# The out-projection of a bidirectional SSD and Conformer layer, written as a software pipeline with a held order, and its state decay moved to ScalarE

## The chip, the cores and the metric

The kernel runs on one core of one Trainium2 chip. The time is that of one execution on the device, in microseconds (us); the median of several runs is compared. Before the change three runs took 1922.21, 1924.39 and 1927.9 us, median 1924.39 us.

## What is computed

One layer of a diffusion backbone over 2304 tokens of width 1024: 256 context tokens and 2048 latent tokens, 18 tiles of 128 tokens. Cut to what matters:

```python
h = rms_norm(x, g_pre) * (1 + scale) + shift
u = h @ w_in
z, xbc, dt_raw, ga, gb, gsil = jnp.split(u, ...)
y_ssd, h_fin = ssd_branch(z, xbc, dt_raw, ...)        # chunked scan, forward and backward, chunks of 128
  ...
  y = (y_f + flip(y_b) + d_skip * xs) * silu(z);  y = rms_norm(y, norm_g)
y_conf = conformer_branch(ga, gb, ...)                # depthwise conv, layer_norm, silu
y_conf = y_conf * silu(gsil)
out = concatenate([y_ssd, y_conf], -1) @ w_out        # 2048 -> 1024
return x + gate * rms_norm(out, g_post), h_fin
```

The backward scan of the SSD branch carries a state from each chunk to the one before it: `state = decay * state + increment`, and the chunk's output takes in `C^T state`. Everything is float32; products use a high and a low part (`h`, `l`) of each operand, so each product is three matmuls: high by high, high by low, low by high.

## The kernel before, in words

The kernel has two stages. The first and longer one makes the in-projection, the convolutions and the forward scan, and leaves per tile in DRAM: `YP` (the SSD output so far), `ZS` and `GS` (gates), `ST` (state increments), `EL` (decay rows), `XB` (the matrix C) and `CV` (the convolved Conformer branch). The second stage, from line 943, is the out-projection with the backward scan, and the change lies there.

The out-projection runs over the 18 tiles in the order 17, 16, ..., 2, 1, 0. For each tile `i` TensorE does 96 matmuls into two PSUM banks `op` (16 blocks `k` of the inner dimension, three products each, two halves of 512 columns; `out_part`, line 1088). Blocks 0 to 7 take the SSD half, `yh` and `yl`; blocks 8 to 15 the Conformer half, `ph` and `pl`. The weights are `woh0` to `woh15` and `wol0` to `wol15`; blocks 9 to 15 of them are loaded, cast and split (`load_wo`, line 952) at the stage's start, through staging buffers `wst` that share their memory with `yh` and `yl`.

What a tile needs ahead of its matmuls:

- SSD half (`ssd_pre`, line 975): loads `ct`, `elb`, `y`, `z`, `stl`; 8 matmuls `qo` of the state `Sb` by `ct`; VectorE multiplies by `elb` (line 993), adds to `y` (994), gates by `z` (995); ScalarE squares (996); VectorE sums eight slices to `zr` (970 to 972). GpSimd then multiplies the state by the decay `eTb` (1003) and adds the increment `stl` (1004).
- Conformer half: load `cn`; VectorE sums eight slices into `cs`; a matmul `cm` with ones spreads the sum over the partitions (1062); VectorE centres (1063); ScalarE squares (1068); VectorE sums to `nq`.
- Norms (lines 1013 and 1026): a matmul `pm` of `zr` and of `nq` by ones, VectorE's `yms`, GpSimd's power -1/2 (line 134), and a matmul `pn` that spreads the two factors over the partitions. VectorE scales `y` (1010) and `cn` (1074); ScalarE casts `yh` (1035), VectorE subtracts `yl` (1036); ScalarE makes eight Silu slices (1076), VectorE gates by `gsl` (1078), ScalarE casts `ph` (1084), VectorE subtracts `pl` (1085).
- Afterwards (`finish`, line 1096): ScalarE squares both `op` banks (1102), VectorE and GpSimd make the factor, VectorE scales (1109), adds the residual `xr` (1113), and SP stores.

The main loop (line 1156) writes these steps for the tile in work, for the next and for the next but one, among the 96 matmuls. The written order isn't what runs: the framework's scheduler orders each engine's instructions by its own forecast of the times, within the data dependencies and the number of buffers of each tag. On the chip every engine then works through its list strictly in that order. The SP queue does the same with the DMAs.

Of the kernel before, what the change touches and what calls it, by code (L numbers as in the profile page):

```python
# [65 lines left out]

@with_exitstack
def backbone_kernel(ctx, tc, xa, xt_in, cols, rows, wconv, conf_b, gp_row, bg_row, state0, w_mod, w_dt, w_in, w_out,
                    y_ctx, y_lat, new_state):
    nc = tc.nc  # L70
    V, S, G, T, DMA = nc.vector, nc.scalar, nc.gpsimd, nc.tensor, nc.sync
# [903 lines left out]
    def ssd_pre(i, first):  # L975
        ct = p1.tile([P, 2, P], F32, tag="ct", name=f"ct{i}", bufs=1)
        DMA.dma_start(ct, xb_slice(i, 10, 2))
        if not first:
# [8 lines left out]
        if not first:
            for g in range(2):
                gs = slice(4 * g, 4 * g + 4)
                po = bank("ss", f"qo{i}{g}")  # L990
                for q in range(4):
                    T.matmul(po[:, q * P:(q + 1) * P], Sb[g][:, q * P:(q + 1) * P], ct[:, g, :], start=True, stop=True)
                V.tensor_tensor(el[:, gs, :], el[:, gs, :], y8(po), MUL)
            V.tensor_tensor(y, y, el, ADD)
        V.tensor_tensor(y, y, z, MUL)
        S.activation(z, y, AF.Square)
        zr = sum8(p1.tile([P, P], F32, tag="zr", name=f"zr{i}", bufs=2), z[:, 0:4, :], z)
        for g in range(2):
            sg = st[:, g * 512:(g + 1) * 512]
            if first:  # L1000
                V.tensor_copy(Sb[g], sg)
            else:
# [29 lines left out]
    def ssd_hl(i, y):  # L1032
        yh = p0.tile([P, 8, P], F32R, tag="yh", name=f"yh{i}", bufs=2)
        yl = p0.tile([P, 8, P], F32R, tag="yl", name=f"yl{i}", bufs=2)
        S.copy(yh, y)  # L1035
        V.tensor_tensor(yl, y, yh.bitcast(F32), SUB)
        return yh, yl
# [20 lines left out]
    def conf_mean(i, n):  # L1058
        t = p2.tile([P, 4, P], F32, tag="cs", name=f"cs{i}", bufs=1)
        t = sum8(t[:, 0, :], t, n)  # L1060
        mean = bank("ss", f"cm{i}")[:, 0:P]
        T.matmul(mean, ones, t, start=True, stop=True)
        V.scalar_tensor_tensor(n, rows8(mean), -1.0 / D, n, MUL, ADD)
        return n

    def conf_square(i, n):
# [4 lines left out]
    def conf_act(i, n, v, pb):
        gs = p2.tile([P, 8, P], F32, tag="gs", name=f"gsl{i}", bufs=1)
        DMA.dma_start(gs, chan_slice(GS, i))
        V.tensor_tensor(n, n, rows8(pb[:, P:2 * P]), MUL)
# [4 lines left out]
        return v

    def conf_hl(i, v):
        ph = p2.tile([P, 8, P], F32R, tag="ph", name=f"ph{i}", bufs=1)
        pl = p2.tile([P, 8, P], F32R, tag="pl", name=f"pl{i}", bufs=1)
        S.copy(ph, v)
        V.tensor_tensor(pl, v, ph.bitcast(F32), SUB)
        return ph, pl

    def out_part(pso, hl, k0, k1, ns=(0, 1)):
        a, b = hl
        for k in range(k0, k1):  # L1090
            for m, (lhs, w) in enumerate(((a, WH[k]), (a, WL[k]), (b, WH[k]))):
                for n in ns:
                    T.matmul(pso[n], lhs[:, k % 8, :], w[:, n * 512:(n + 1) * 512],  # L1093
                             start=(k == 0 and m == 0), stop=(k == 15 and m == 2))

    def finish(i, pso, halves):
        x = p3.tile([P, D], F32, tag="xr", name=f"xr{i}", bufs=1)
        DMA.dma_start(x, xa[i * P:(i + 1) * P, :])
# [5 lines left out]
        V.tensor_scalar(ms[:, 0:1], ms[:, 0:1], 1.0 / D, EPS, MUL, ADD)
        r = rstd_of(p3, ms[:, 0:1], f"or{i}")
        g = gg[1 if i < NCTX else 0]
        for n in range(2):
            cs = slice(n * 512, (n + 1) * 512)
            V.scalar_tensor_tensor(o[:, cs], pso[n], r, g[:, cs], MUL, MUL)
            if halves:  # L1110
                V.tensor_tensor(o[:, cs], o[:, cs], x[:, cs], ADD)
        if not halves:
            V.tensor_tensor(o, o, x, ADD)
        dst = y_ctx[i * P:(i + 1) * P, :] if i < NCTX else y_lat[(i - NCTX) * P:(i - NCTX + 1) * P, :]
        for cs in (slice(0, 512), slice(512, D)) if halves else (slice(0, D),):
            DMA.dma_start(dst[:, cs], o[:, cs])

# [8 lines left out]
    yz = ssd_pre(i, False)  # L1126
# [27 lines left out]
    yz = ssd_pre(order[1], False)  # L1154
    n = conf_mean(order[1], conf_load(order[1]))
    for a, i in enumerate(order):
        last = a + 1 == NT
        nxt = None if last else order[a + 1]
        pt = conf_hl(i, v)
        banks(i)  # L1160
        if not last:
            v, nq = conf_square(nxt, n)
        out_part(pso[i], yh, 0, 2)
        if not last:
            rs = norms(nxt, yz, (v, nq))
        y = yz[0]
        if a + 2 < NT:
            n2 = conf_load(order[a + 2])
            yz = ssd_pre(order[a + 2], order[a + 2] == NCTX - 1)
# [8 lines left out]
        out_part(pso[i], pt, 9, 11)
        if a + 2 < NT:
            n = conf_mean(order[a + 2], n2)  # L1180
        if last:
            out_part(pso[i], pt, 11, 16, (0,))
            out_part(pso[i], pt, 11, 16, (1,))
        else:
            out_part(pso[i], pt, 11, 16)
# [1 line left out]
        if i == 1:
            load_gg(1)
        finish(i, pso[i], last)
# [61 lines left out]
```

## Time and profile before

| | |
|---|---|
| median of three runs | 1924.39 us |
| profiled execution: its time, its span | 1922.83 us, 1921.1 us |
| TensorE busy | 1827.8 us, 95% of the span, 11223 matmul records |
| VectorE, ScalarE, GpSimd busy | 1207.8, 799.6, 267.0 us |
| mean granted TensorE clock | 0.976 |
| longest group on the chain that ended last | `op`, line 1093, 18% of the span |

In rows of the profile PE is TensorE, PEld its weight load, DVE VectorE, ACT ScalarE, POOL GpSimd, SP the DMA queue's engine. A row of the timeline gives start, duration, engine, line, operation, output and inputs, the number of instructions merged, and in brackets how long the engine sat idle ahead and what released it. Matmul records overlap: the distance of the starts is what one costs. A row of a window gives its length, the busy time of each engine with the count of records, the granted clock (1.00 is full), the share of the DMA engines and GB/s. Some matmul records are missing.

### The profile page before, as it was taken

The page shows a single profiled execution, that of the slowest core. Times are in us where ns is not written, and L with a number is a line of the kernel's source. Part 1 is how long each engine was busy: PE and PEld are TensorE (multiplying, and loading weights), DVE is VectorE, ACT ScalarE, POOL GpSimd, SP SyncE. Part 2 cuts the span into 40 slices and gives each one's busy share as a digit, 9 for nine tenths or more (in the row PEclk, how much of TensorE's full clock was granted, in tenths as well). Part 3 has the DMA queues.
Part 4 walks back from the last instruction along what each step waited for, and adds up shares of the span by engine and source line. Part 5 has one row for each costly group of instructions (what it writes and reads, how often), then busy time and mean ns, then how long its engine had stood idle before and what let it go on. Part 6 is the DMA issues. An engine that isn't in the chain of part 4 may idle for free.

```text
span 1921.1 us, 29715 instructions
## 1 busy us (share of the span) xinstructions
PE 1827.8 (95%) x11223; PEld 1506.3 (78%) x11223; DVE 1207.8 (63%) x1807; ACT 799.6 (42%) x1684; POOL 267.0 (14%) x349
## 2 busy tenths in 40 slices
PE   7899999999999999999998899999988989898998
PEld 5788887787888888888876678778867877777776
DVE  2487978784555543587589555753367666757662
ACT  3656424454545432744245455642233332323331
POOL 0002001111101000100011111100123313323120
PEclk8899999999999999999999999999999999999999
DMA  8556666575666653555888888869666556456522
GB/s 302 202 208 218 220 205 201 193 255 168 235 204 205 223 189 122 195 175 179 214 201 227 218 226 260 244 197 288 232 188 185 155 143 181 130 142 174 166 70 73
DMA packets 305579, 375.34 MB, mean 195 GB/s; under 512 B 85270, under 2 KB 204950, under 8 KB 305436
## 3 DMA queue, kind: packets, MB, share of 16 engines
q1 hardware_dynamic: 284700, 335.69, 56.3%
q10 hardware_dynamic: 20736, 37.76, 6.8%
q8 instruction: 88, 1.44, 0.3%
q14 instruction: 55, 0.45, 0.1%
HBM read 243.79 MB, written 129.59 MB: 194 GB/s over the span
## 4 chain that ended last, share of the span: by engine, by line
PE 82%; DMA 6%; DVE 6%; issue 3%; ACT 2%; POOL 0%; SPq 0%; POOLq 0%; DVEq 0%; ACTq 0%
PE op L1093 18%; PE sp L377 7%; PE sp L378 7%; PE sp L379 7%; PE xp L377 5%; PE xp L378 5%; PE xp L379 5%; PE ga L377 3%; PE ga L379 3%; PE ga L378 3%; PE gb L377 3%; PE gb L379 3%; PE gb L378 3%; PE py L718 2%; PE po L725 2%
## 5 line engine op out<-in xcount | busy, mean ns | idle before, releaser
L682 ACT ACTIVATE lb<-lb,WB 128x128 f32<-128x128 f32 x576 | 184.7, 392 | 168.3 <-POOL lb L674 153.5
L377 PE MATMUL sp<-hh,wh 128*128 128x512 f32 (+1 forms) x640 | 238.5, 373 | 0.0
L378 PE MATMUL sp<-hl,wh 128*128 128x512 f32 (+1 forms) x640 | 236.2, 369 | 0.0
L379 PE MATMUL sp<-hh,wl 128*128 128x512 f32 (+1 forms) x640 | 236.0, 369 | 0.0
L674 POOL TENSOR_SCALAR_AFFINE_SELECT lb<-lb 128x512 f32<-128x512 f32 x144 | 111.7, 780 | 713.1 <-ACT el L671 349.1
L377 PE MATMUL xp<-hh,wh 128*128 128x512 f32 (+1 forms) x480 | 178.5, 373 | 5.1 <-ACT wh L352 2.9
L379 PE MATMUL xp<-hh,wl 128*128 128x512 f32 (+1 forms) x480 | 178.4, 372 | 0.0
L378 PE MATMUL xp<-hl,wh 128*128 128x512 f32 (+1 forms) x480 | 178.3, 372 | 0.0
L474 DVE SCALAR_TENSOR_TENSOR cva<-raw,cwh,cva 128x1280 f32<-128x1280 f32 (+1 forms) x96 | 141.7, 1484 | 18.1 <-ACT cva L468 16.0
L379 PEld LDWEIGHTS sp<-hh,wl 128*128 128x128 f32 x640 | 120.7, 189 | 20.7
L377 PEld LDWEIGHTS sp<-hh,wh 128*128 128x128 f32 x640 | 120.7, 189 | 20.5 <-DVE sth L554 0.2
L378 PEld LDWEIGHTS sp<-hl,wh 128*128 128x128 f32 x640 | 120.8, 189 | 19.7
L377 PE MATMUL ga<-hh,wh 128*128 128x512 f32 (+1 forms) x320 | 122.2, 382 | 5.7 <-DMA wh<-whd 5.7
L377 PE MATMUL gb<-hh,wh 128*128 128x512 f32 (+1 forms) x320 | 121.4, 379 | 6.4 <-DVE gth L541 6.4
L1093 PE MATMUL op<-woh,yh 128*128 128x512 f32 x288 | 95.7, 410 | 26.3 <-ACT yh L1035 26.1
L379 PE MATMUL ga<-hh,wl 128*128 128x512 f32 (+1 forms) x320 | 119.8, 374 | 0.5 <-DMA wl<-wld 0.5
L378 PE MATMUL ga<-hl,wh 128*128 128x512 f32 (+1 forms) x320 | 119.7, 374 | 0.0
L379 PE MATMUL gb<-hh,wl 128*128 128x512 f32 (+1 forms) x320 | 119.6, 374 | 0.0
L378 PE MATMUL gb<-hl,wh 128*128 128x512 f32 (+1 forms) x320 | 119.6, 374 | 0.0
L554 DVE SCALAR_TENSOR_TENSOR sth<-sth,sp 128x512 f32<-128x512 f32 (+1 forms) x80 | 50.5, 631 | 103.9 <-ACT sth L553 99.1
L377 PEld LDWEIGHTS xp<-hh,wh 128*128 128x128 f32 x480 | 91.6, 191 | 22.3 <-ACT wh L352 3.6
L594 DVE SCALAR_TENSOR_TENSOR cg<-cg,cv 128x256 f32<-128x256 f32 x240 | 107.8, 489 | 0.6
(224 smaller groups left out, 3820.6 us busy)
## 6 DMA issues: line engine op xcount, KB each, us to landing
lb<-lt ACTq DMA_DIRECT2D x144, 256.0 KB, 4.5
wr<-in_w_in SPq DMA_DIRECT2D x88, 256.0 KB, 4.6
whd<-wh SPq DMA_DIRECT2D x44, 512.0 KB, 3.4
wld<-wl SPq DMA_DIRECT2D x44, 512.0 KB, 5.6
wh<-whd SPq DMA_DIRECT2D x44, 512.0 KB, 4.9
wl<-wld SPq DMA_DIRECT2D x44, 512.0 KB, 5.7
xT<-xb SPq DMA_DIRECT2D x18, 512.0 KB, 5.4
yp<-yg SPq DMA_DIRECT2D x36, 256.0 KB, 4.3
```

What stands on the lines that cost most here:

```text
L377: T.matmul(ps[:, :BN], wh[:, k, :], hh[:, k, :], start=(k == 0), stop=False)
L378: T.matmul(ps[:, :BN], wh[:, k, :], hl[:, k, :], start=False, stop=False)
L379: T.matmul(ps[:, :BN], wl[:, k, :], hh[:, k, :], start=False, stop=(k == KT - 1))
L474: V.scalar_tensor_tensor(a[:, :n], raw[:, t:t + n], cwh[:, ct * 5 + t:ct * 5 + t + 1], a[:, :n], MUL, ADD)
L554: V.scalar_tensor_tensor(th, th, 1.0, ps[:, :BN], ADD, MUL)
L594: V.scalar_tensor_tensor(acc, g[:, t:t + 256], cv[:, w0 + t:w0 + t + 1], acc, MUL, ADD)
L674: G.affine_select(E[g, hq, d], E[g, hq, d], pattern=[[0, 4], [sg, P]], compare_op=ALU.is_ge, fill=NEG, base=0, channel_multiplier=-sg)
L682: S.activation(lb[:, h, :], lb[:, h, :], AF.Exp, bias=WB[:, i, c + h:c + h + 1])
L718: T.matmul(py[g][j * HD:(j + 1) * HD, q * P:(q + 1) * P], xt[g][:, h * HD:(h + 1) * HD], E[g, hq, 0][:, t, :], start=True, stop=True)
L725: T.matmul(po[g][:, q * P:(q + 1) * P], Sf[g][:, q * P:(q + 1) * P], bc[:, 2 + g, :], start=True, stop=True)
L1093: T.matmul(pso[n], lhs[:, k % 8, :], w[:, n * 512:(n + 1) * 512], start=(k == 0 and m == 0), stop=(k == 15 and m == 2))
```

## The change

Three things are done, all in the out-projection.

First, the steps are cut into smaller functions (`ssd_load`, `st_load`, `state_mm`, `state_decay`, `state_add`, `y_state`, `y_gate`, `y_sum`, `conf_sum`, `conf_centre`, `finish_squares`, ...), and the loop writes them out at chosen places among the matmuls. Matmuls of tile `i` carry beside them the norms, scaling, casts and Silu of the next tile, the state, gating and centring of the next but one, and the finish of the tile before. The loads of `ct`, `elb`, `y`, `z` and `cn` are written three tiles ahead.

Secondly, `V`, `S` and `T` become wrappers (`InOrder`): while `on` is set, which is in the main loop, the scheduler must keep each engine's instructions in the written order. GpSimd and the DMAs on SP stay free, and so does all that is written ahead of the loop.

Thirdly, the state's decay goes from GpSimd (one multiplication of 128x512 per half) to ScalarE (eight activations `Copy` of 128x64 with a scale per half, 16 a tile), and the addition of the increment from GpSimd to VectorE. GpSimd keeps the powers.

Buffers: `o` and `v` get two, `zr` and `nq` one, `ph` and `pl` stay at one; `cs` goes, its sums lie in `v`.

```diff
+class InOrder:
+    def __getattr__(self, name):
+        f = getattr(self._eng, name)
+        if not self.on:
+            return f
+        return lambda *a, **k: self._tc.keep_in_program_order(f(*a, **k))
...
-    V, S, G, T, DMA = nc.vector, nc.scalar, nc.gpsimd, nc.tensor, nc.sync
+    G, DMA = nc.gpsimd, nc.sync
+    V, S, T = (InOrder(tc, e) for e in (nc.vector, nc.scalar, nc.tensor))
...
-                G.tensor_tensor(b3(Sb[g]), b3(Sb[g]), bh(eTb[:, i, g * 8:(g + 1) * 8]), MUL)
-                G.tensor_tensor(Sb[g], Sb[g], sg, ADD)
+    def state_decay(i, g):
+        if i != NCTX - 1:
+            for h in range(8):
+                cs = slice(h * HD, (h + 1) * HD)
+                S.activation(Sb[g][:, cs], Sb[g][:, cs], AF.Copy, scale=eTb[:, i, 8 * g + h:8 * g + h + 1])
+    def state_add(i):
...
+                V.tensor_tensor(Sb[g], Sb[g], sg, ADD)
...
+    V.on = S.on = T.on = True
     for a, i in enumerate(order):
...
         banks(i)
+        pt = hl(p2, "p", 1, i, v)
+        out_part(pso[i], yh, 0, 1)
+        rs = None if last else norms(nxt, yz, nq)
+        if a:
+            finish_squares(order[a - 1])
+        lo(pt)
+        out_part(pso[i], yh, 1, 4)
+        if nxt is not None:
+            state_add(nxt)
+            pb = spread(nxt, rs)
+        if nx2 is not None:
+            st_load(nx2)
+            v2, t = conf_sum(nx2, n2)
+        if a:
+            finish_power(order[a - 1])
+        out_part(pso[i], yh, 4, 5)
+        if nx2 is not None:
+            state_mm(nx2)
+        if nxt is not None:
...
+            ssd_scale(nxt, y, pb)
+            yhn = hl(p0, "y", 2, nxt, y)
+            conf_scale(n, pb)
...
+            conf_silu(n, v)
+        out_part(pso[i], yh, 5, 8)
+        if nx2 is not None:
+            mean = conf_mean(nx2, t)
+        if nxt is not None:
+            lo(yhn)
+        if a:
...
+            finish_gate(order[a - 1])
+        out_part(pso[i], pt, 8, 10)
+        if nx2 is not None:
+            y_state(nx2)
+            state_decay(nx2, 0)
+            conf_centre(n2, mean)
+            conf_square(v2, n2)
+        if nxt is not None:
+            conf_gate(v, gs)
+        if nx2 is not None:
+            y_gate(nx2)
+            state_decay(nx2, 1)
+            gs = gs_load(nx2)
+            nq = conf_sqsum(nx2, v2)
+        if a:
+            finish_add(order[a - 1])
+        if nx2 is not None:
+            yz = y_sum(nx2)
+        if a + 3 < NT:
+            ssd_load(order[a + 3])
+            n, n2 = n2, conf_load(order[a + 3])
...
+            out_part(pso[i], pt, 10, 16)
```

Below, the numbers behind a name are the tile or block (`op10_0` is the first bank of tile 10, `yh9` the high part of tile 9) and a counter of the framework. On TensorE before the change, at the border of tile 10 and tile 9, the scheduler had put the spreading matmuls `pn9` between the last blocks of tile 10:

```order
L1093 MATMUL op10_1_15156<-wol14_13722,ph10_15151 128x512
L1029 MATMUL pn9_15246<-ident_209,yr90_15180 128x128
L1062 MATMUL cm8_15300<-cs8_15296,ones_218 128x128
L1029 MATMUL pn9_15246<-ident_209,yr91_15184 128x128
L1093 MATMUL op10_0_15155<-woh14_13723,pl10_15152 128x512
L1093 MATMUL op10_1_15156<-woh14_13723,pl10_15152 128x512
L1093 MATMUL op10_0_15155<-woh15_13729,ph10_15151 128x512
L1093 MATMUL op10_1_15156<-woh15_13729,ph10_15151 128x512
L1093 MATMUL op10_0_15155<-wol15_13728,ph10_15151 128x512
L1093 MATMUL op10_1_15156<-wol15_13728,ph10_15151 128x512
L1093 MATMUL op10_0_15155<-woh15_13729,pl10_15152 128x512
L1093 MATMUL op10_1_15156<-woh15_13729,pl10_15152 128x512
```

Eight matmuls of tile 10 stand behind `pn9`, and then the first matmul that reads `yh9`, which is made from `pn9`. After the change, in tile 9's own matmuls, `pn8` for the tile after stands behind block 3, and the state's product `qo7` behind block 4:

```order
L77 MATMUL op9_0_15480<-woh3_13142,yl9_15351 128x512
L77 MATMUL op9_1_15481<-woh3_13142,yl9_15351 128x512
L77 MATMUL pn8_15529<-ident_209,yr80_15496 128x128
L77 MATMUL pn8_15529<-ident_209,yr81_15500 128x128
L77 MATMUL op9_0_15480<-woh4_13168,yh9_15350 128x512
L77 MATMUL op9_1_15481<-woh4_13168,yh9_15350 128x512
L77 MATMUL op9_0_15480<-wol4_13167,yh9_15350 128x512
L77 MATMUL op9_1_15481<-wol4_13167,yh9_15350 128x512
L77 MATMUL op9_0_15480<-woh4_13168,yl9_15351 128x512
L77 MATMUL op9_1_15481<-woh4_13168,yl9_15351 128x512
L77 MATMUL qo70_15548<-ct7_15433,Sb0_13062 128x128 x4
L77 MATMUL qo71_15549<-ct7_15433,Sb1_13063 128x128 x4
```

`pn` has moved from 8 matmuls ahead of the tile that needs it to 72 ahead of it. The second place is the start of the out-projection on TensorE. Before, the first bank of tile 17 follows the last in-projection matmul `sp` at once:

```order
L379 MATMUL sp1_4640_7_4_13620<-hh4_7330,wl5536_1_13453 128x512
L1093 MATMUL op17_0_13783<-woh0_13065,yh17_13570 128x512
L1093 MATMUL op17_0_13783<-wol0_13064,yh17_13570 128x512
L1093 MATMUL op17_0_13783<-woh0_13065,yl17_13571 128x512
L1093 MATMUL op17_0_13783<-woh1_13091,yh17_13570 128x512
L1093 MATMUL op17_0_13783<-wol1_13090,yh17_13570 128x512
```

After, the small matmuls written ahead of the loop come first, and behind block 0 stands `pm16`, which needs the sums of tile 16:

```order
L393 MATMUL sp1_4640_7_4_13634<-hh4_7330,wl5536_1_13467 128x512
L1059 MATMUL pm17_13676<-ones_218,nq17_13672 128x1
L1070 MATMUL pn17_13682<-ident_209,yr171_13680 128x128
L1014 MATMUL qo160_13762<-ct16_13749,Sb0_13062 128x128 x4
L1014 MATMUL qo161_13763<-ct16_13749,Sb1_13063 128x128 x4
L1107 MATMUL cm16_13801<-v16_13797,ones_218 128x128
L77 MATMUL op17_0_13822<-woh0_13065,yh17_13584 128x512
L77 MATMUL op17_1_13823<-woh0_13065,yh17_13584 128x512
L77 MATMUL op17_0_13822<-wol0_13064,yh17_13584 128x512
L77 MATMUL op17_1_13823<-wol0_13064,yh17_13584 128x512
L77 MATMUL op17_0_13822<-woh0_13065,yl17_13585 128x512
L77 MATMUL op17_1_13823<-woh0_13065,yl17_13585 128x512
```

What could run at the start without tile 16, 48 matmuls of blocks 0 to 7 in the order before, is now 6 matmuls of block 0. On VectorE, in front of the sums for that `pm16`, the list after the change reads (`wol9` and `wol10` are the low parts of weight blocks 9 and 10):

```order
L1134 SCALAR_TENSOR_TENSOR v17_13594<-v17_13594,gsl17_13685 128x1024
L976 TENSOR_TENSOR wol9_13705<-wst9_13707,woh9_13706 128x1024
L976 TENSOR_TENSOR wol10_13711<-wst10_13713,woh10_13712 128x1024
L984 TENSOR_TENSOR v16_13797<-v16_13797 128x512
L984 TENSOR_TENSOR z16_13756<-z16_13756 128x512
L985 TENSOR_TENSOR v16_13797<-v16_13797 128x256
L985 TENSOR_TENSOR z16_13756<-z16_13756 128x256
L986 TENSOR_TENSOR nq16_13805<-v16_13797 128x128
L986 TENSOR_TENSOR zr16_13777<-z16_13756 128x128
L976 TENSOR_TENSOR wol11_13717<-wst11_13719,woh11_13718 128x1024
L77 TENSOR_SCALAR yms160_13836<-pm16_13833 128x1
L77 TENSOR_SCALAR yms161_13840<-pm16_13833 128x1
```

The gate of tile 17, which needs the load `gsl17`, and two weight splits now stand ahead of the sums of tile 16, and a third split ahead of `yms16`. Up to the last in-projection matmul TensorE's list is the same before and after, but for the name of one buffer.

More of the change, by code (lines that the diff above doesn't have):

```diff
@@ new lines, in st_load, with state_mm @@
+    def st_load(i):
+        sl[i]["st"] = p1.tile([P, D], F32, tag="st", name=f"stl{i}", bufs=1)
+        DMA.dma_start(sl[i]["st"], ST[i])
+    def state_mm(i):
+        if i != NCTX - 1:
+            sl[i]["po"] = [bank("ss", f"qo{i}{g}") for g in range(2)]
+            for g, po in enumerate(sl[i]["po"]):
+                for q in range(4):
+                    T.matmul(po[:, q * P:(q + 1) * P], Sb[g][:, q * P:(q + 1) * P], sl[i]["ct"][:, g, :],
+                             start=True, stop=True)
@@ L995, in ssd_pre, with y_sum @@
         V.tensor_tensor(y, y, z, MUL)
         S.activation(z, y, AF.Square)
[L997 to L1002, printed above, removed]
-                G.tensor_tensor(b3(Sb[g]), b3(Sb[g]), bh(eTb[:, i, g * 8:(g + 1) * 8]), MUL)
-                G.tensor_tensor(Sb[g], Sb[g], sg, ADD)
-        return y, zr
+    def y_sum(i):
+        z = sl[i]["z"]
+        zr = p1.tile([P, P], F32, tag="zr", name=f"zr{i}", bufs=1)
+        return sl[i]["y"], sum8(zr, z[:, 0:4, :], z)
@@ L1125, in backbone_kernel @@
     run(take(blocks, 5))
-    yz = ssd_pre(i, False)
+    ssd_load(i)
+    st_load(i)
+    state_mm(i)
+    y_state(i)
+    y_gate(i)
+    yz = y_sum(i)
+    for g in range(2):
+        state_decay(i, g)
+    state_add(i)
     run(take(blocks, 5))
@@ L1153, in backbone_kernel @@
     load_gg(0)
-    yz = ssd_pre(order[1], False)
-    n = conf_mean(order[1], conf_load(order[1]))
+    i = order[1]
+    ssd_load(i)
+    st_load(i)
+    n = conf_load(i)
+    state_mm(i)
+    y_state(i)
+    y_gate(i)
+    yz = y_sum(i)
+    for g in range(2):
+        state_decay(i, g)
+    v2, t = conf_sum(i, n)
+    conf_centre(n, conf_mean(i, t))
+    nq = conf_sqsum(i, conf_square(v2, n))
+    gs = gs_load(i)
+    ssd_load(order[2])
+    n2 = conf_load(order[2])
+    V.on = S.on = T.on = True
@@ L1156, in backbone_kernel @@
     for a, i in enumerate(order):
         last = a + 1 == NT
-        nxt = None if last else order[a + 1]
-        pt = conf_hl(i, v)
+        nxt = order[a + 1] if a + 1 < NT else None
+        nx2 = order[a + 2] if a + 2 < NT else None
         banks(i)
[L1161 to L1169, printed above, removed]
@@ L1184, in backbone_kernel @@
         else:
[L1185 removed]
+            out_part(pso[i], pt, 10, 16)
             yh = yhn
[L1187 to L1189 removed]
+    finish_squares(i)
+    finish_power(i)
+    finish_gate(i)
+    finish_add(i, True)
+    V.on = S.on = T.on = False
     state_out(1, Sb, lambda n: p1.tile([P, D], F32, tag="z", name=n, bufs=2)[:, 0:512])
```

144 lines of the change are left out of this document (81 added, 63 removed).

## The prediction

> **What bounds the kernel now.** I read the stretches first: the in-projection, the first two tiles of the out-projection, and its other sixteen, from the first matmul of tile 15 to the last of tile 0.
>
> ```profile
> 1100.00:1400.00 300.00, 300.00 (x2725) 241.79 (x2725) 163.98 (x244) 130.96 (x296) 36.72 (x42) 1.00 0.81 239
> 1402.30:1474.03 71.73, 57.37 (x268) 46.66 (x266) 53.91 (x66) 29.17 (x47) 21.37 (x18) 0.90 0.67 193
> 1474.03:1913.70 439.67, 409.71 (x1901) 342.01 (x1899) 277.11 (x384) 131.15 (x248) 108.95 (x98) 0.96 0.50 139
> ```
>
> After the length come the busy times of PE, PEld, DVE, ACT and POOL, then the granted clock. The in-projection has no gap on PE and the full clock. In the sixteen tiles PE is idle for 439.67 - 409.71 = 30.0 us, and the clock is below 1. The waits of PE in that stretch say for whom:
>
> ```profile
> PE op L1093 <- ACT yh L1035: 20.8, 9, 3.3
> PE op L1093 <- DVE yl L1036: 4.7, 2, 2.4
> PE op L1093 <- DVE oms L1104: 4.3, 2, 2.1
> ```
>
> So PE waits at the border of two tiles for the next tile's `yh` and `yl`. One border, on PE, shows the chain and what follows it:
>
> ```profile
> 1578.97 0.38 PE L1029 MATMUL pn<-ident,yr 128*128 128x128 f32 x2
> 1579.19 0.39 PE L1062 MATMUL cm<-cs,ones 128*128 128x128 f32 x2
> 1579.42 0.39 PE L1029 MATMUL pn<-ident,yr 128*128 128x128 f32 x2
> ...
> 1583.10 0.74 PE L1093 MATMUL op<-woh,yh 128*128 128x512 f32 x2 [2.83 <-ACT yh L1035]
> 1583.67 0.62 PE L1093 MATMUL op<-wol,yh 128*128 128x512 f32 x2
> 1584.14 0.28 PE L1018 MATMUL pm<-ones,zr 128*128 128x1 f32 x2
> 1584.28 3.57 PE L992 MATMUL qo<-ct,Sb 128*128 128x128 f32 x16
> 1587.50 0.90 PE L1093 MATMUL op<-woh,yl 128*128 128x512 f32 x2
> 1588.24 0.62 PE L1093 MATMUL op<-woh,yh 128*128 128x512 f32 x2
> ...
> 1591.88 0.39 PE L1093 MATMUL op<-woh,yl 128*128 128x512 f32 x1
> ```
>
> `pn` is done at 1579.6. VectorE then centres and scales, ScalarE casts, and at 1583.10 PE goes on. The product `qo` after the gap takes 3.22 us from start to start (1584.28 to 1587.50); without a gap ahead of it it takes 1.70:
>
> ```profile
> 1477.00 1.95 PE L992 MATMUL qo<-ct,Sb 128*128 128x128 f32 x16
> 1478.70 0.47 PE L1093 MATMUL op<-woh,yh 128*128 128x512 f32 x1
> ```
>
> PE is thus slowed to about half for some us after each stall. At full clock the 16 `op` matmuls from 1588.24 to 1591.88 cost 3.64 / 16 = 0.2275 us each. From the same rows `pn` costs 2 x 0.22, `cm` 0.23, `pm` 2 x 0.14. The sixteen tiles hold 1536 `op` (349.4 us), and in the order after 13 `qo` (22.1), 15 `pn` (6.6), 14 `cm` (3.2) and 15 `pm` (4.2): 385.5 us of work. Before, one `qo` more lies in the stretch, so its 439.67 are 387.2 of work, 30.0 of idling and 22.5 of slowed work.
>
> **The change, part by part.**
>
> *Steady tiles.* With `pn` behind block 3 the chain to the next `yh` has 72 matmuls, 16.4 us, of cover, where it had 8. What can be late next is the sum `zr` ahead of `pm`, because PE must now do `pm` behind block 0: behind a late `pm` 90 matmuls queue that don't need it. VectorE's list per tile, priced by starts in a stretch where GpSimd was idle:
>
> ```profile
> 1594.52 0.68 DVE L970 TENSOR_TENSOR cs<-cn 128x512 f32<-128x512 f32 x1
> 1595.12 1.21 DVE L1085 TENSOR_TENSOR pl<-v,ph 128x1024 fp32r<-128x1024 f32 x1
> 1596.25 1.21 DVE L995 TENSOR_TENSOR y<-y,z 128x1024 f32<-128x1024 f32 x1
> 1597.39 0.41 DVE L971 TENSOR_TENSOR cs<-cs 128x256 f32<-128x256 f32 x1
> 1597.72 0.68 DVE L970 TENSOR_TENSOR v<-v 128x512 f32<-128x512 f32 x1
> 1598.33 0.28 DVE L972 TENSOR_TENSOR cs<-cs 128x128 f32<-128x128 f32 x1
> 1598.53 0.41 DVE L971 TENSOR_TENSOR v<-v 128x256 f32<-128x256 f32 x1
> ```
>
> Nine of 128x1024 at 1.13 (10.2), seven of 128x512 at 0.60 with the two moved state additions (4.2), three tails of sums at 0.33 + 0.20 (1.6), the finish's two scalings (1.3) and four tiny ones (0.6): 17.9 us. The list starts when `pm` is read, at 1.9 us of the tile's clock. It waits some 0.7 for `pn` (on PE at 6.2) and 1.5 for ScalarE's casts and squares, so `zr` of the following tile is there at 22, and its `pm` is due at 24.5 + 1.4 = 25.9 (24.5 is 96 x 0.2275 and one `qo`, `pn`, `cm` and `pm`). Slack 4 us.
>
> ScalarE has 131.15 / 16 = 8.2 us of work per tile and gets 16 activations of 128x64. None is in the trace; the nearest rows bound it, one without and one with a per-partition operand:
>
> ```profile
> L444 ACT ACTIVATE lr<-pl 128x128 f32<-128x128 f32 x4 | 0.9, 268 | 1.1 <-DVE lr L443 1.1
> L682 ACT ACTIVATE lb<-lb,WB 128x128 f32<-128x128 f32 x576 | 184.7, 392 | 168.3 <-POOL lb L674 153.5
> ```
>
> At 0.27 to 0.39 us they add 4.3 to 6.3, and ScalarE holds 12.5 to 14.5 of 24.5 us; I take 0.35, nearer to the row with the operand. The first eight lie between Silu and the square that waits for the centring, the others after the last square, so at either end they stay covered by PE; without that cover they would cost their 5.6 us. GpSimd loses its state work; only its powers remain on the path, covered by blocks 1 to 3.
>
> SP's list per tile becomes `xr`, `z`, `stl`, `ct`, `y`, `cn`, `elb`, `gsl`, store, each waiting for a buffer.
>
> ```profile
> gsl<-gs SPq DMA_DIRECT2D x14, 512.0 KB, 6.1
> stl<-st SPq DMA_DIRECT2D x13, 512.0 KB, 6.1
> cn<-cv SPq DMA_DIRECT2D x13, 512.0 KB, 4.9
> ```
>
> By these landing times `stl` can leave at 4.5 (after the state additions) and is due at 27.8; `cn` leaves at 12 (after Silu) and is due at 28.9; `gsl` leaves at 16.2 and is due at 39. The least slack is 12 us. So the sixteen tiles cost no wait: 385.5 instead of 439.7, a gain of 54.2, of which 22.5 hang on the clock.
>
> [...]
>
> *The start.* It gets worse. The in-projection's last matmul gives way at 1402.3, where the second stretch begins. `pm17`, its power and `pn17` take 1.2 us, `qo16`, `cm16` and block 0 take 3.3: 1406.9. Then `pm16` waits for `zr16`, which stands on VectorE behind the gate of tile 17, which waits for `gsl17`, which waits for the last write of GS:
>
> ```profile
> 1403.86 5.41 DMA gs<-sth
> ...
> 1414.82 4.17 DMA wst<-in_w_out
> ...
> 1423.51 9.73 DMA wst<-in_w_out
> ```
> ```profile
> wst<-in_w_out SPq DMA_DIRECT2D x7, 512.0 KB, 7.8
> ...
> gsl<-gs SPq DMA_DIRECT2D x4, 512.0 KB, 5.9
> ```
>
> 1409.3, and 5.9 to land: 1415.2; gate 1.1, two weight splits 2.3, sums 2.3: `pm16` at 1421. PE idles 14 us where before it had 42 more matmuls to do and idled 5.2; and it starts slowly after a long gap:
>
> ```profile
> 1421.05 1.22 PE L1093 MATMUL op<-woh,ph 128*128 128x512 f32 x2 [5.18 <-ACT ph L1084]
> ...
> 1427.67 0.63 PE L1093 MATMUL op<-woh,ph 128*128 128x512 f32 x2
> ```
>
> (fourteen matmuls in 6.6 us there, some 3 us lost). Blocks 1 to 3 end at 1428. Meanwhile the staging buffers pass the weights one after another: wst11 leaves when `wol9` is made (1417.6), and load, cast and split take 7.8 + 2.3; so blocks 11, 13 and 15 are split at 1427.7, 1437.8 and 1447.9. `yms16` stands behind the first, `cm15`'s sums behind the second, `yl16` behind the third. PE gets through `pn16` at 1429.3, `cm15` at 1438.7, and ends tile 17 at 1449.6. Tile 16's block 0 ends at 1451; `zr15` comes 8.5 us of VectorE's list after `yl16` (1449.0), so `pm15` at 1457.6, a stall of 6.5 and 3 of slow clock, and tile 15 begins at 1483.5. If loads land in 4.2 us, PE's own work and one stall give 1472; at 9.7 us, 1489. I take 1482, near the median of the loads: 8 us later than the 1474.03 of before.
>
> *The end.* From the last matmul's start to the span's end it is 7.8 us in both orders (1913.33 to 1921.1):
>
> ```profile
> 1913.33 0.39 PE L1093 MATMUL op<-woh,pl 128*128 128x512 f32 x1
> ...
> 1917.52 0.94 SPq L1116 DMA_DIRECT2D out<-o  x2
> ```
>
> The final state's 8 transposes and two copies fall in there now, beside VectorE's last steps: 0 to 1 us, taken as 0.
>
> *The sum.* Span 1921.1 + 8 - 54.2 = 1874.9. The profiled execution took 1922.83 and lies 1.6 under the median of 1924.39; the same difference of 46.2 from the median gives 1878.
>
> **The rivals.**
>
> *Slowed work stays.* If something else than the gaps lowers the clock in this stage, the 22.5 us stay: 1878 + 22.5 = 1901. [...] Against it stand the 300 us without a gap at a granted clock of 1.00, and the slow `qo` right behind a gap.
>
> *A longer start.* The held lists couple the weight splits with the sums, and every load there competes. If each of the first two tiles loses one load more (9.7 us), tile 15 begins 20 us later: 1898. For it: the 71.73 us of the first two tiles already hold 14.4 of idling. Against: fewer than three loads in a row can stand ahead of any matmul.
>
> *VectorE's held list is late in each tile (slower).* Place: `pm`, behind block 0. If a load, a cast or GpSimd's power comes late, VectorE can no longer pass it, and `zr` comes after 25.9. Each us beyond is a us of PE's, and a stall of 2 us brought a slow stretch of 1.5 (the `qo` above). The loop's gain per tile is 54.2 / 16 = 3.4, less 0.5 for the start: a list 5.4 us longer than my 22, that is 27.4, eats all of it; at 29 us it is 16 x 1.6 = 26 us slower: 1950. Before, VectorE needed 277.11 / 16 = 17.3 us of work per tile and had free choice; that, and 4 us of slack, speaks against.
>
> *It does nothing.* The order might be held and the waits merely move, each tile's stall as long as now, at another matmul: 1924. The order on TensorE has moved, so this needs VectorE's list at just 27 us.
>
> **How the numbers follow.** Forecast 1878, chance 0.68; alone its range is 1866 to 1890 (start from -2 to +15, up to 5 us of small waits). Slowed work stays 0.07; longer start 0.14; VectorE late 0.06, of which 0.05 slower; nothing 0.05, of which 0.03 within 0.3%. A measurement of this kernel tells 0.3% (6 us) from no change. Faster by more: 0.92, within: 0.03, slower: 0.05. The range leaves out the slower cases and half of the 1901: 1864 to 1902.
>
> **What would show it.** Right: the sixteen tiles in 384 to 392 us, PE idle under 5 us in them, granted clock 1.00, `qo` at 1.7 throughout, no wait for `yh`; `pm16` waiting some 14 us at 1407 to 1421 and `pm15` some 6; ScalarE's activations of 128x64 at 0.27 to 0.39. Wrong: PE waiting at `pm` in each tile (VectorE's list over 25 us), at `qo` for the state (ScalarE's decay late), or a clock under 0.98 without gaps; or the first two tiles over 95 us.

## The result and the profile after

The changed kernel takes 1873.74 us (median of 4 runs, 1872.07 to 1875.25), the kernel before 1926.14 us beside it (1922.21 to 1928.67): a ratio of 0.9729, 95% interval 0.9708 to 0.9751. The forecast was 1878 us; as a gain it was 46 us, and 52 were measured. The profiled execution took 1872.28 us, its span is 1870.5 us (before 1922.83 and 1921.1), so the span has lost 50.6 us.

The windows of the changed kernel, with the columns of the prediction's table: the first two tiles, from the end of the in-projection's last matmul (by its row, 0.17 us after the next one starts) to the first matmul of tile 15, and the sixteen tiles from there to the start of the last matmul of tile 0.

```profile
1405.07:1472.40 67.33, 54.19 (x266) 45.60 (x266) 52.93 (x73) 41.45 (x96) 5.35 (x6) 0.90 0.77 206
1472.40:1862.61 390.21, 390.21 (x1892) 327.95 (x1891) 272.46 (x409) 178.96 (x453) 40.72 (x46) 1.00 0.55 155
```

The sixteen tiles have no idle PE left and the full granted clock, where before 30 us of idling stood at a clock of 0.96. All waits of PE behind the in-projection are now these two, both in the first tile:

```profile
PE pm L77 <- DVE zr L986: 12.3, 1, 12.3
PE pn L1070 <- POOL yr L148: 0.9, 1, 0.9
```

One tile on PE, from its `pm` to the next. (L77 is the line of the helper that holds the order; all held instructions bear it.)

```profile
1498.60 0.28 PE L77 MATMUL pm<-ones,zr 128*128 128x1 f32 x2
1498.74 0.36 PE L77 MATMUL pm<-ones,nq 128*128 128x1 f32 x2
1498.96 0.72 PE L77 MATMUL op<-woh,yh 128*128 128x512 f32 x2
1499.52 0.63 PE L77 MATMUL op<-wol,yh 128*128 128x512 f32 x2
...
1503.18 0.61 PE L77 MATMUL pn<-ident,yr 128*128 128x128 f32 x4
...
1505.02 1.95 PE L77 MATMUL qo<-ct,Sb 128*128 128x128 f32 x16
1506.72 0.70 PE L77 MATMUL op<-woh,yh 128*128 128x512 f32 x2
...
1523.44 0.28 PE L77 MATMUL pm<-ones,zr 128*128 128x1 f32 x2
```

The period is 1523.44 - 1498.60 = 24.84 us, and `qo` takes 1.70 (1505.02 to 1506.72). In the same tile VectorE is done with `zr` at 1518.75, 4.7 us ahead of `pm`, and until it can read `pm` it waits 5.22 us; ScalarE's eight decays of one half take 2.01 us:

```profile
1518.46 0.29 DVE L77 TENSOR_TENSOR zr<-z 128x128 f32<-128x128 f32 x1
1523.97 0.23 DVE L77 TENSOR_SCALAR yms<-pm 128x1 f32<-128x1 f32 x2 [5.22 <-PE pm L77]
```
```profile
1509.37 2.01 ACT L77 ACTIVATE Sb<-Sb,eTb 128x64 f32<-128x64 f32 x8
```

The start, on PE and on VectorE: `pm16` waits for `zr16`, which stands behind the gate of tile 17 (which waits for `gsl`) and two weight splits.

```profile
1422.20 0.56 PE L77 MATMUL pm<-ones,zr 128*128 128x1 f32 x2 [12.26 <-DVE zr L986]
1423.05 1.20 PE L77 MATMUL op<-woh,yh 128*128 128x512 f32 x2
...
1428.66 0.61 PE L77 MATMUL pn<-ident,yr 128*128 128x128 f32 x4
```
```profile
1416.28 1.23 DVE L1134 SCALAR_TENSOR_TENSOR v<-v,gsl 128x1024 f32<-128x1024 f32 x1 [3.70 <-DMA gsl<-gs]
1417.42 2.36 DVE L976 TENSOR_TENSOR wol<-wst,woh 128x1024 fp32r<-128x1024 f32 x2
...
1421.77 0.28 DVE L986 TENSOR_TENSOR zr<-z 128x128 f32<-128x128 f32 x1
```

Where the 50.6 us went, from start to start of the matmuls that bound the stages: the in-projection's last matmul started 2.6 us later (1404.67 for 1402.09), the first two tiles, from there, lost 4.2 (71.94 to 67.73), the sixteen tiles lost 49.1 (1913.33 - 1474.03 = 439.30 to 390.21), and the end, from the last matmul's start at 1862.61 to 1870.5, grew by 0.1. Sum: 2.6 - 4.2 - 49.1 + 0.1 = -50.6.

### The profile page after: what moved, and what is told of

Same layout as the page of the kernel before. It is cut to its first block, busy times and chain, and to the rows that moved or that the text cites. A ratio compares the mean times of both kernels' runs of the same rounds, so it can differ in the third digit from the quotient of the medians.

```text
span 1870.5 us, 30012 instructions
## 1 busy us (share of the span) xinstructions
PE 1808.1 (97%) x11223; PEld 1493.1 (80%) x11223; DVE 1203.1 (64%) x1841; ACT 863.8 (46%) x1956; POOL 175.9 (9%) x281
## 4 chain that ended last, share of the span: by engine, by line
PE 85%; DMA 7%; DVE 4%; ACT 1%; issue 1%; SPq 1%; POOL 0%; POOLq 0%; DVEq 0%; ACTq 0%
PE op L77 21%; PE sp L391 7%; PE sp L392 7%; PE sp L393 7%; PE xp L391 5%; PE xp L392 5%; PE xp L393 5%; PE ga L391 3%; PE ga L393 2%; PE ga L392 2%; PE gb L391 2%; PE gb L393 2%; PE gb L392 2%; DMA lb<-lt 2%; PE py L732 2%; DVE cg L608 2%
## 5 line engine op out<-in xcount | busy, mean ns | idle before, releaser
L391 PEld LDWEIGHTS sp<-hh,wh 128*128 128x128 f32 x640 | 120.6, 189 | 20.8 <-DVE sth L568 0.4
L392 PEld LDWEIGHTS xp<-hl,wh 128*128 128x128 f32 x480 | 91.7, 191 | 15.7 <-DVE hl L312 0.4
```

What stands on the lines that cost most here:

```text
L391: T.matmul(ps[:, :BN], wh[:, k, :], hh[:, k, :], start=(k == 0), stop=False)
L392: T.matmul(ps[:, :BN], wh[:, k, :], hl[:, k, :], start=False, stop=False)
```

## The experiments

**Which of the three parts pays.** Four kernels ask it. The first lets all three engines be ordered by the scheduler, with the loop as the change writes it:

```diff
-    V.on = S.on = T.on = True
+    V.on = S.on = T.on = False
```

> The changed kernel with its new loop and the decay on ScalarE, but with no engine held to the written order. TensorE's order is then, in a steady tile, pm behind the first four matmuls of the second half, pn 22 matmuls later, and 22 more, qo and cm ahead of the next tile's yh. Theory 'the loop as written' (the norms are asked for an iteration early, whoever orders them): from pm to yr the changed kernel's trace shows 2.9 us and from pn to yh 2.8 us; 22 matmuls cover 5.0 and 7.0 us, so the sixteen tiles stay at 385 to 400 us with less than 10 us of waiting for yh, and tile 17's first half is no longer behind pm16: 1860 to 1882 in all. Rival 'the held order': without it the borders wait as before the change (20 us for yh, some slowed work): 1900 to 1925.

Measured: 1880.33 us (1879.62 to 1882.06), ratio 0.979 (0.9769 to 0.9812). All its waits of PE behind the in-projection:

```profile
PE op L1141 <- ACT ph L1076: 7.4, 1, 7.4
PE op L1141 <- ACT yh L1076: 6.4, 2, 3.4
PE op L1141 <- DVE yl L1080: 3.7, 1, 3.7
```

These are four waits: three in the first two tiles (7.4, 3.4, 3.7) and one of 2.9 near the end; the tiles between have none. There the scheduler, given this loop, puts 22 matmuls, `qo` and `cm` between `pn` and the next `yh`, and the period is 24.98 us. So the loop as written, with its buffers and the decay on ScalarE, brings 40.6 us (1920.95 - 1880.33), and the rival falls. The buffers were not tested apart from the loop.

The second holds TensorE alone:

```diff
-    V.on = S.on = T.on = True
+    T.on = True
```

> The changed kernel with TensorE alone held to the written order; VectorE and ScalarE are ordered by the scheduler. Theory 'TensorE's order is what pays': VectorE has 5 us of slack at pm in each tile, so its order may shift by that much for nothing: 1868 to 1880. Rival 'VectorE must be held too': another order puts a step of the next tile behind one that waits, pm or yh then waits 2 us or more in each of 16 tiles and TensorE slows after each wait: 1900 or more.

Measured: 1873.79 us (1870.93 to 1874.58), ratio 0.9752 (0.9726 to 0.9778), within the spread of the changed kernel. Holding VectorE and ScalarE brings nothing; holding TensorE brings the 6.5 us between these two kernels. Their profiles say where. The first two tiles take as long in both (70.5 and 70.3 us from the last in-projection matmul to tile 15), though the waits differ. From tile 15 to the last matmul it is 396.1 us without and 390.8 with the order held, and 4.3 of these 5.4 lie in the last four tiles, where the wait of 2.9 is. The rest is the in-projection's end, 1.7 us later in the free kernel.

The third puts the state back on GpSimd, with all orders held:

```diff
-            for h in range(8):
-                cs = slice(h * HD, (h + 1) * HD)
-                S.activation(Sb[g][:, cs], Sb[g][:, cs], AF.Copy, scale=eTb[:, i, 8 * g + h:8 * g + h + 1])
+            G.tensor_tensor(b3(Sb[g]), b3(Sb[g]), bh(eTb[:, i, g * 8:(g + 1) * 8]), MUL)
...
-                V.tensor_tensor(Sb[g], Sb[g], sg, ADD)
+                G.tensor_tensor(Sb[g], Sb[g], sg, ADD)
```

> The changed kernel with all orders held, but with the state's decay and addition back on GpSimd. Theory 'the decay was not in the way': GpSimd's work of 6 us per tile slows VectorE while it runs (before the change 128x1024 steps beside the addition took 2.3 us where others took 1.2, some 3 us more per tile), less the 1.2 us of additions that VectorE loses; the 5.2 us for which VectorE waits at pm take that up, and the time stays at 1870 to 1880. Rival 'ScalarE's decay is needed': VectorE's list passes the slack or qo waits for the state, 2 us or more in each of 16 tiles: 1900 or more.

Measured: 1872.84 us (1871.93 to 1873.97), ratio 0.975 (0.9729 to 0.9771): no difference. GpSimd's addition and VectorE beside it, in one tile:

```profile
1509.92 3.53 POOL L1027 TENSOR_TENSOR Sb<-Sb,stl 128x512 f32<-128x512 f32 x2
```
```profile
1510.60 1.70 DVE L77 TENSOR_TENSOR y<-y,elb 128x1024 f32<-128x1024 f32 x1
...
1524.64 0.22 DVE L77 TENSOR_SCALAR yms<-pm 128x1 f32<-128x1 f32 x2 [5.03 <-PE pm L77]
```

One VectorE step is 0.5 us longer beside the addition (1.70, elsewhere 1.22), less than I expected from the 2.3 us of such steps before (at 1590.04 and 1592.29, beside additions from 1589.00 to 1593.51), and VectorE still waits 5.03 us for `pm`.

The fourth is the kernel before with the decay on ScalarE and the addition on VectorE, and nothing else:

```diff
-                G.tensor_tensor(b3(Sb[g]), b3(Sb[g]), bh(eTb[:, i, g * 8:(g + 1) * 8]), MUL)
-                G.tensor_tensor(Sb[g], Sb[g], sg, ADD)
+                for h in range(8):
+                    cs = slice(h * HD, (h + 1) * HD)
+                    S.activation(Sb[g][:, cs], Sb[g][:, cs], AF.Copy, scale=eTb[:, i, 8 * g + h:8 * g + h + 1])
+                V.tensor_tensor(Sb[g], Sb[g], sg, ADD)
```

> The kernel before with one part of the change only: decay on ScalarE, addition on VectorE. TensorE's order at the border of two tiles stays (pm, 22 matmuls, pn, 4 to 9 matmuls, then the wait). Theory 'the border's order bounds': the chain pn, centring, scaling, cast ran while GpSimd was idle, so the waits for yh stay at 20 us or more and the time within 10 us of the kernel before. Rival 'GpSimd's load was the bound': VectorE is relieved of the slow steps beside GpSimd and the gain is 20 us or more.

Measured: 1932.00 us (1925.36 to 1934.87) beside 1920.95, ratio 1.0047 (1.0028 to 1.0066): slower by 0.5%, by the medians 11 us, just past the 10 I had set. `yh` is waited for 33.2 us in the stretch of the sixteen tiles, where it was 20.8:

```profile
PE op L1095 <- ACT yh L1037: 33.2, 13, 3.3
```

One border shows one way. On VectorE `y` starts at 1617.34 and is done when the next step starts, at 1618.47; ScalarE has just begun seven decays, and the cast comes behind them:

```profile
1617.34 1.21 DVE L1012 TENSOR_TENSOR y<-y,pn 128x1024 f32<-128x1024 f32 x1
1618.47 1.22 DVE L1076 TENSOR_TENSOR cn<-cn,pn 128x1024 f32<-128x1024 f32 x1
```
```profile
1618.56 1.77 ACT L1005 ACTIVATE Sb<-Sb,eTb 128x64 f32<-128x64 f32 x7
1620.23 1.03 ACT L1037 CAST yh<-y 128x1024 fp32r<-128x1024 f32 x1
```

Seven of the 13 waits, 14.6 us together, have seven or more decays right ahead of the cast like this one. At the other six (18.6 us) no decay stands there. At five of these, 3.30 us each, the scheduler has put no `op` at all between `pn` and the next `yh`; before the change that was so at three borders:

```profile
1645.80 0.39 PE L1031 MATMUL pn<-ident,yr 128*128 128x128 f32 x2
1649.48 0.99 PE L1095 MATMUL op<-woh,yh 128*128 128x512 f32 x2 [3.30 <-ACT yh L1037]
```

So TensorE's order didn't quite stay, and the longer waits are in part the decays in front of the cast and in part another order of the scheduler. The move of the decay brings no gain here, and no difference where the loop leaves slack; it is not what pays.

**How much slack VectorE has.** The step that makes `yl` is repeated, four or seven times more:

```diff
-            lo(yhn)
+            for _ in range(5):
+                lo(yhn)
```

> The changed kernel with VectorE's subtraction that makes yl done five times instead of once in each tile (four more steps of 1.13 us, 4.5 us; the value is the same). In the changed kernel VectorE waits 5.2 us per tile for pm. Theory 'slack of 5 us': the list still ends ahead of pm, nothing waits: within 6 us of the changed kernel, 1868 to 1880. Rival 'no real slack' (something else on the list is already tight, such as the gate's load or the state): 2 us or more per tile, 1905 or more.

Measured: 1882.74 us (1880.77 to 1883.50), ratio 0.9783 (0.9755 to 0.981); a little above my bound. In the steady tiles the theory holds: `zr` ends just ahead of `pm`, and the period is 25.07 on average.

```profile
1631.14 0.29 DVE L77 TENSOR_TENSOR zr<-z 128x128 f32<-128x128 f32 x1
1632.13 0.22 DVE L77 TENSOR_SCALAR yms<-pm 128x1 f32<-128x1 f32 x2 [0.70 <-PE pm L77]
```

Most of what it costs stands in the start, where `pm15` waited 5.5 us for `zr` (in the changed kernel VectorE waited only 1.55 us for that `pm`): in the profiles the first two tiles are 8.6 us longer, and the sixteen 3.1.

> The same with seven more steps, 7.9 us per tile, 2.7 us beyond the slack: the place of my rival 'VectorE's held list is late'. Theory 'each us beyond is a us of TensorE's and the gap slows it': pm waits some 2.7 us in each of 15 or 16 tiles (40 us), and the 18 matmuls behind it take up to 1.5 us longer, which VectorE, waiting for pn, passes on: 1913 to 1940. Rival 'VectorE catches up' (the delay is taken back, since the steps wait for nothing else): under 1895. PE's waits should all stand at pm.

Measured: 1971.41 us (1969.61 to 1974.03), ratio 1.0246 (1.0216 to 1.0276): slower than the kernel before, and 31 us above my range. Every tile waits at `pm`:

```profile
PE pm L77 <- DVE zr L77: 64.2, 16, 8.0
```

One of these borders on PE, and what VectorE does with it:

```profile
1610.01 0.59 PE L77 MATMUL pm<-ones,zr 128*128 128x1 f32 x2 [3.76 <-DVE zr L77]
1610.89 1.20 PE L77 MATMUL op<-woh,yh 128*128 128x512 f32 x2
...
1617.06 0.60 PE L77 MATMUL pn<-ident,yr 128*128 128x128 f32 x4
```
```profile
1617.70 1.22 DVE L77 TENSOR_TENSOR y<-y,pn 128x1024 f32<-128x1024 f32 x1 [2.44 <-PE pn L77]
...
1620.04 10.04 DVE L77 TENSOR_TENSOR yl<-y,yh 128x1024 fp32r<-128x1024 f32 x8
```

The repeated steps took 10.04 / 8 = 1.25 us each, not 1.13, so 8.8 us were added, 4.1 beyond the slack of 4.7; the wait at `pm` is 3.8. Behind it the 18 matmuls up to `pn` took 6.2 us instead of 4.2, and VectorE, the late engine, waited 2.44 us for `pn` instead of 0.48. The tile takes 31.3 us (1610.01 to 1641.31 at the next `pm`): 24.84, 3.8 of waiting and 2.6 of slowed work, which comes back as lateness. I had priced the gap without most of that.

**Whether the gap slows what follows.** In these two, `pn` stands behind the tile's last matmul, and what needs it behind it; the second has PE work in the gap, on unused columns of the bank of `cm`:

```diff
-            pb = spread(nxt, rs)
...
+            out_part(pso[i], pt, 10, 16)
+        if nxt is not None:
+            pb = spread(nxt, rs)
```
```diff
+            if nx2 is not None:
+                for _ in range(22):
+                    T.matmul(cmb[nx2][:, 256:512], WL[0][:, 0:P], WL[0][:, 0:256], start=True, stop=True)
```

> The changed kernel with all orders held, but pn asked for behind the tile's last matmul instead of behind block 3, with the scalings and casts that need it behind it on VectorE and ScalarE. PE has nothing to do from pn to yh, some 2.6 us by the changed kernel's rows (pn to the scaling 0.65, scaling 1.2, cast 1.1, less pn's own 0.44), then 0.3 for yl, in 16 tiles: 46 us. Theory 'a gap slows what follows': another 1.5 us per tile, 1935 to 1950. Rival 'a gap costs its own length': 1915 to 1925. Rival 'the place of pn doesn't matter': under 1890.

> The same with 22 matmuls more per tile (128x256, about 0.114 us each, 2.5 us together; their result is not used) between pn and the next tile's yh, in 15 tiles or so: PE waits as long for yh in all, but works in the gap. Theory 'a gap slows what follows': no slowed stretch now, granted clock 1.00, and the time is shorter than that of the kernel with the empty gap by 1 to 2 us per tile, 1912 to 1925. Rival 'the slow stretch comes from something else at the border': the same time as with the empty gap.

Measured: with the empty gap 1959.45 us (1934.88 to 1963.78), ratio 1.0157 (1.0088 to 1.0225), above my range; with the gap filled 1922.24 us (1918.50 to 1926.94), ratio 0.9985 (0.9968 to 1.0002). The filled gap saves 37 us, 2.3 per tile, though PE does more: the 22 matmuls in one gap took 2.72 us (1613.15 to 1615.87), 0.124 each, where I had put 0.114. The same stretch of both, empty first:

```profile
1480.00:1860.00 380.00, 351.32 (x1509) 287.60 (x1509) 235.41 (x350) 152.21 (x389) 21.00 (x39) 0.89 0.49 141
```
```profile
1480.00:1860.00 380.00, 379.12 (x1956) 320.88 (x1955) 257.81 (x386) 166.98 (x423) 22.62 (x42) 1.00 0.53 153
```

The granted clock goes from 0.89 to 1.00 by nothing but work in the gap. That the slow stretches come from the gaps is thus shown. How long they are isn't fixed by the code: three of the four runs with the empty gap took 1958.59 to 1963.78 us at a mean granted clock of 0.962 or 0.963, the fourth 1934.88 us at 0.974. By an estimate from these clocks 0.038 of a span of 1956.9 us is lost, 74 us, and 0.026 of 1933.2, 50 us; the 24 us between them are the whole difference to the profiled run of 1958.59. One border with the empty gap:

```profile
1626.34 0.61 PE L77 MATMUL pn<-ident,yr 128*128 128x128 f32 x4
1629.34 0.73 PE L77 MATMUL op<-woh,yh 128*128 128x512 f32 x2 [2.39 <-ACT yh L77]
1629.91 0.84 PE L77 MATMUL op<-wol,yh 128*128 128x512 f32 x2
1630.60 1.22 PE L77 MATMUL op<-woh,yl 128*128 128x512 f32 x2
...
1635.89 1.05 PE L77 MATMUL op<-wol,yh 128*128 128x512 f32 x2
1636.74 0.73 PE L77 MATMUL op<-woh,yl 128*128 128x512 f32 x2
```

The gap begins at 1626.95; the first pair behind it starts 0.57 us ahead of the next; from 1630.60 to 1636.74 the pairs of `op` start 0.85 to 1.02 us apart, from 1637.31 on some 0.46. This slow stretch costs 3.5 us (the period is 30.7: 24.84, 2.39 and the rest), where I had taken 1.5.

**A better start.** In tile 17 all of the first half goes ahead of `pm16`, and blocks 8 and 9 ahead of `pn16`; the second kernel has `pm15` behind block 3 of tile 16, too:

```diff
-        out_part(pso[i], yh, 0, 1)
+        k0, k1, k2 = ((8, 8, 8), (4, 7, 7))[a] if a < 2 else (1, 4, 5)
+        out_part(pso[i], yh, 0, k0)
...
-        out_part(pso[i], yh, 1, 4)
+        out_part(pso[i], yh, k0, k1)
+        if not a:
+            out_part(pso[i], pt, 8, 10)
```

> The changed kernel once more, unchanged, beside the next two: 1869 to 1878.

> The changed kernel with another order in tile 17 alone: all 48 matmuls of the first half ahead of pm16 (before: 6), then blocks 8 and 9, then pn16. Theory 'the start loses what pm16 waits for zr16' (12.3 us of waiting and a slow stretch): the first half runs from 1408.3 to 1419.2, pm16 waits 3 us, tile 16 begins near 1437.5 instead of 1447.6. But pm15 then stands at 1439, and zr15 comes 15 us behind pn16, at 1442: 3 us of waiting and some slowed work there, so 4 to 7 us of the 10 are left: 1866 to 1870. Rival 'the weights pace the start' (the last of them is split at 1437 to 1438): tile 17's second half waits for them and 0 to 3 us are gained: 1871 to 1875.

> The same, and in tile 16 pm15 behind block 3 instead of block 0, with three more blocks ahead of pn15. Theory: the 18 matmuls (4.1 us) cover VectorE's lateness at zr15, and tile 15 begins 8 to 10 us earlier than the 1472.4 of the changed kernel: 1863 to 1867, below the one with tile 17 alone. Rival 'the weights pace the start': as there, 1871 to 1875.

Measured: the changed kernel again 1871.87 us (1869.17 to 1874.39, 5 runs), ratio 0.9738 (0.972 to 0.9756); tile 17 alone 1867.73 us (1866.24 to 1872.77), 0.9719 (0.97 to 0.9737); both 1867.52 us (1864.12 to 1868.89), 0.971 (0.9693 to 0.9727). The last has the lowest median of this study: its runs all lie under those of the changed kernel, by 4.4 us between the medians, though the intervals of the ratios overlap. From tile 17 alone it can't be told (0.2 us between the medians). Tile 15 begins some 4 us earlier, counted from the in-projection's end; that is half of what I expected, and the median lies 0.5 us above my range. From `pn17` to the `pm` in the first block of tile 15 it takes 1465.62 - 1402.27 = 63.35 us, in the changed kernel 1473.76 - 1406.06 = 67.70: the same 4.35. What is left are two gaps of over 1 us, and no matmul waits for a weight itself:

```profile
PE pm L77 <- DVE zr L986: 3.1, 1, 3.1
PE op L77 <- DVE pl L77: 2.3, 1, 2.3
```

But the second gap is a weight's all the same. `pl17` stands on VectorE behind the split of block 11, which waited 2.85 us for its cast (and the cast 4.25 us for the load):

```profile
1421.51 1.23 DVE L976 TENSOR_TENSOR wol<-wst,woh 128x1024 fp32r<-128x1024 f32 x1 [2.85 <-ACT woh L975]
...
1422.78 1.21 DVE L77 TENSOR_TENSOR pl<-v,ph 128x1024 fp32r<-128x1024 f32 x1
```

So VectorE's order around `zr16` and `pl17` paces the start, and through it the load `gsl17` at the first gap and a weight at the second; the rival's place, tile 17's second half, was right in this. PE was slow behind both gaps: from 1419.65 to 1427.63 the pairs of `op` start 0.85 to 1.02 us apart where no gap lies between. How many us an order without these splits ahead of `pl17` would save was not tested. The kernel with tile 17 alone stays open: its profile, of its slowest run, shows 68.9 us for that way, with three such gaps (3.0, 2.9, 2.2), while its other three runs gained 4 us.

## Why the prediction was right, and which terms were off

*The waits at the border.* Right. `pn` behind block 3 leaves no wait for `yh` or `yl` in 16 tiles, and with `pn` back at the border they return (2.39 us a tile, 1959.45 us). The experiments narrow it: what does it is that the norms of the next tile are asked for early in the loop; of the held orders only TensorE's has a worth of its own, 6.5 us, most of it near the end.

*The slowed work goes with the gaps.* Right: granted clock 1.00, `qo` at 1.70, and the filled gap shows the cause. The rival of 1901, slowed work that stays, is out. "After each stall" said too much: in the sixteen tiles of the kernel before, nine of the eleven gaps of over 1 us have a granted clock of 0.50 behind them, but behind those of 2.35 us (PE goes on at 1558.20) and 2.14 us (1732.30) it stayed at 1.00.

*The size of the loop.* Off by 4.7: 390.2 instead of 385.5. I priced every `op` at 0.2275 us. In the tile shown above the first pair behind `pm` takes 0.56 (1498.96 to 1499.52) and the pair behind `qo` 0.55 (1506.72 to 1507.27), where a pair elsewhere takes 0.455; behind `pn` and `cm` it is 0.54. Four changes of shape at some 0.09 are 0.37 us per tile; `pm`, `pn` and `cm` themselves took 0.36, 0.37 and 0.14, together 0.08 less than priced. That gives 0.3 of the 0.34 by which 24.84 is longer than 24.5. By the same measure the slowed work before was some 17 us rather than 22.5, since part of it was this. The prediction's own table says as much: at a granted clock of 0.96 over 439.67 us, 0.04 x 439.67 = 17.6 us are lost.

*The start.* This step failed, though the total came out: "the staging buffers pass the weights one after another", 7.8 us a load, with tile 15 at 1482, 8 us later than before. It began at 1472.40, and from the in-projection's last matmul the two tiles are 4.2 us shorter than before instead of 8 longer. Up to `pn16` the steps came near what was worked out (`pm16` at 1422.20 for 1421, blocks 1 to 3 done at 1428.66 for 1428), from an in-projection that ended 2.6 us later. Then the splits of blocks 11, 13 and 15, put at 1427.7, 1437.8 and 1447.9, started at 1424.80, 1430.77 and 1436.79. The loads in that stretch landed in 5.0 us, and two were in flight at once:

```profile
wst<-in_w_out SPq DMA_DIRECT2D x5, 512.0 KB, 5.0
```

So VectorE was early, `cm15` and `pm15` didn't wait, and my lower end (1472, with loads of 4.2 us) came true by the clock. The trace of before could have told me: its seven splits go through the same buffers, with loads of 7.8 us, and the last of them starts at 1434.34:

```profile
1434.34 1.23 DVE L962 TENSOR_TENSOR wol<-wst,woh 128x1024 fp32r<-128x1024 f32 x1 [3.72 <-ACT woh L961]
```

There the first split is done at 1412.55, and the last starts 21.8 us later. My chain had 30.3 us for the same links (1417.6 to 1447.9), and I hadn't held it against that row.

*VectorE's list and ScalarE's decay.* Right in kind. `zr` is done 4.7 us ahead of `pm` where I had 4 of slack, and the added 5.0 us just used it up. The decays follow each other at 2.01 / 8 = 0.25 us, under my lower bound of 0.27. That bound and the upper one were mean durations of one instruction, and by this measure a decay took 0.334 us, inside them; since they overlap, the start to start is what counts. It changed nothing, since ScalarE had room.

*The slower rival.* Its place was right, its price too low: a wait of 3.8 us in each tile came to 98 us (1971.41 against 1873.74), 6.1 per tile, where 16 x 3.8 gives 61. The difference is the slowed work behind each gap (2.6 us in the tile shown).

*What the sum hid.* The span came 4.4 us under the 1874.9 worked out, nearer than the terms were: 12.2 too much for the start (1482 - 1402.09 = 79.91, measured 67.73), 4.7 too little for the loop, 0.1 for the end, and 2.6 for an in-projection that ended later. Another 0.4 was counted twice: the 439.67 of before runs to the end of the last matmul, and the end's 7.8 from its start. That the errors partly cancel is luck; with the start's alone the forecast would have missed by 12 us. The in-projection is spread: its last matmul started at 1404.7 and 1403.4 in the two profiles of the changed kernel, and from 1398.3 to 1404.9 in all profiles here.

## What to carry to other kernels

Where an engine waits at each border for a chain through two others, ask for the chain's first link as early as its input allows; once that is done, who does the side work and who holds the order may matter little, and one kernel for each part tells. A short gap on TensorE mostly cost more than its length here (one of 2.39 us cost 3.5 us more, though two of the eleven in the kernel before had no slow stretch behind them), so count it with the slow stretch, and remember that a late engine which waits for TensorE is made later by it (VectorE waited 2.44 us for `pn` instead of 0.48). Hold a chain worked out from single durations against the whole chain as the trace before shows it.

## What the runs showed of the hardware

- The slow stretch began 3.0 us after the gap's start in the rows below, not at its end, and a gap of 1.77 us was enough. In the kernel before with the decay alone moved, PE goes on at 1621.32, is slow from the third pair at 1622.58, 3.0 us after the gap began (1621.32 - 1.77 = 1619.55), and fast again from 1626.03. The four pairs in between start 0.73 to 1.02 us apart, those behind 0.45 to 0.47:

```profile
1621.32 0.73 PE L1095 MATMUL op<-woh,yh 128*128 128x512 f32 x2 [1.77 <-ACT yh L1037]
1621.89 0.63 PE L1095 MATMUL op<-wol,yh 128*128 128x512 f32 x2
1622.58 1.22 PE L1095 MATMUL op<-woh,yl 128*128 128x512 f32 x2
...
1626.03 0.63 PE L1095 MATMUL op<-woh,yh 128*128 128x512 f32 x2
```

- From its first slow pair to the next fast one the stretch lasted 3.4 us there (1622.58 to 1626.03) and 6.7 us behind the gap of 2.39 us (1630.60 to 1637.31). Behind the gap of 2.83 us in the kernel before, the granted clock was 1.00 up to 1584.1, 0.50 from 1585.1 to 1587.1 and 1.00 again from 1588.1. What sets these lengths, no run tells.
- The first pair of 128x512 matmuls behind a matmul of another shape takes 0.54 to 0.56 us instead of 0.455 (one tile of the changed kernel).
- ScalarE's activations of 128x64 follow each other at 0.25 us (2.01 us for eight, changed kernel). Beside GpSimd's addition a VectorE step of 128x1024 took 2.3 us in the kernel before and 1.7 in the changed loop with the state on GpSimd; why less there, no run tells.
